# Two transformer blocks on one core: the end of the squared-relu MLP with joined norm weights, an unscaled VectorE sum, and the residual scaled a stage later

## Chip, cores and metric

One core of one Trainium2 chip. The metric is the device time of one execution in microseconds, the median of several runs; lower is better. The kernel before takes 2157.38 us (three runs, 2157.03 to 2157.44). A profile of one execution of it stands beside that.

## The reference, cut to what matters

Two blocks follow each other on 512 tokens of width 1024. The change lies where the first ends and the second begins. The first block's MLP squares a relu, its result goes through a final norm, and the second block norms that again ahead of its short convolution:

```python
    h = rmsnorm(x, norm_ffn[l])
    x = x + jnp.square(jax.nn.relu(h @ w_ff1[l])) @ w_ff2[l]
    return rmsnorm(x, final_norm)
...
            xn = rmsnorm_2(x, attn_norm[l])
            x = x + short_conv_mixer(xn, a_w_in[l], a_conv[l], a_w_out[l])
```

With s the MLP's sum per token, r1 its inverse root mean square, and fin and attn the two weight vectors (one number for each of the 1024 features), the residual that goes on is s * fin * r1, and the second norm is s * fin * attn * r1 * r2, with r2 from the mean square of s * fin * r1. So two sums of squares are wanted: that of s, and that of s * fin.

## The kernel before

Activations lie with features on partitions: x is eight tiles of 128 features by 512 tokens, f32. All products are f32 by splitting: each operand is cut into a high part (xh, wh) and the rest (xl, wl), and each chunk of 128 features takes three matmuls (lines 202 to 204). mm_T makes one product, 128 outputs by 512 tokens, in eight chunks, so 24 matmuls. Weights come as 1 MB chunks through SP's queue into four raw buffers, each chunk holding two units; prep cuts a unit into wh (ScalarE) and wl (VectorE) two units ahead of its use, into room for three units. A load goes out when a raw buffer is free, that is after the wl that read it last. PSUM has eight banks, one a product.

The framework plans the order of each engine's instructions by a simulated timeline; each engine then runs its own list in order, and waits on semaphores. So the order in the code is not always the order on an engine: matmuls of two or three products may be mixed.

The MLP runs in four groups g (lines 912 to 924). Each makes eight products f1 with relu, square and split, and then eight products f2; of each of those VectorE takes t = product * rb2 (tile rs, line 918), and GpSimd adds it to x[i] (line 919). In the last group, g = 3, more follows for each i: the square of x[i] into acc1; x[i] times fin on VectorE (line 922); the square of that into acc2; and split with attn as scale (lines 475 to 483), which gives the pair xh (ScalarE, line 120) and xl (VectorE, line 110). Squares are ScalarE's (sq), their sums GpSimd's (acc, line 107). These eight pairs XN are the right operands of the conv stage.

The conv stage (lines 947 to 973) makes products ac, ah, ab for i = 0 to 7. After the second product stats_x is emitted (lines 927 to 935: ones-matmuls ss, line 439, over acc1 and acc2, then short VectorE and ScalarE operations on 128x4 for r1 and r1 * r2), after the third bcast_x (lines 937 to 943: matmuls bc, line 455, spread two such vectors over the partitions as rb and rbx, rbb is rb squared, and GpSimd multiplies each x[i] by rbx). Then got_c, got_h and got_b take the products; x itself is read again only at the stage's end, by the ao products' sums (line 880).

Of the kernel before, what the change touches and what calls it, by code (L numbers as in the profile page):

```python
# [8 lines left out]
F32 = mybir.dt.float32  # L9
# [4 lines left out]
ALU = mybir.AluOpType  # L14
# [8 lines left out]
NEG = -1e30  # L23
FF = 4096
FF2 = 2816
# buffers: raw weights, split weights, 2 KB tiles, small tiles, pairs of tiles, tiles of the attention
N_RAW = 4
N_W = 6
N_T = 54
N_S = 10  # L30
N_T2 = 6
XA = 14
# units of weights split ahead of their use
LOOK = 2
# recurrence: products of the gates beside it, levels of decays ahead, start and pace beside the
# products, levels at which the head before is normed, levels whose product is GpSimd's
N_FILL = 3
AHEAD = 4
HGSTART = 36
HGW = (130, 76)  # L40
CS = (0, 2, 6)
MUL_POOL = (1, 3)
# attention: steps from scores to the turn and on to the values, queries ahead, order of queries
# and gates, start and pace beside the products, steps of a product at which norms go on, blocks
# of queries that GpSimd divides
LAG = 4
VLAG = 3
QL = 3
# [9 lines left out]
def tile_two_blocks(ctx: ExitStack, tc: tile.TileContext, a: dict, out: bass.AP):  # L58
    nc = tc.nc
    act, dve, pool, pe = nc.scalar, nc.vector, nc.gpsimd, nc.tensor  # L60

    cp = ctx.enter_context(tc.tile_pool(name="const", bufs=1))
# [43 lines left out]
    def tt(e, o, i0, i1, op=ALU.mult):  # L106
        e.tensor_tensor(out=o, in0=i0, in1=i1, op=op)  # L107

    def stt(o, i0, s, i1, op0, op1):
        dve.scalar_tensor_tensor(out=o, in0=i0, scalar=s, in1=i1, op0=op0, op1=op1)  # L110

    def ts(e, o, i, s1, op0, s2=None, op1=None):
        if s2 is None:
            e.tensor_scalar(out=o, in0=i, scalar1=s1, scalar2=None, op0=op0)  # L114
        else:
            e.tensor_scalar(out=o, in0=i, scalar1=s1, scalar2=s2, op0=op0, op1=op1)
# [5 lines left out]
    def pieces(t, n):  # L122
        return t.rearrange("p (b i) -> p b i", i=n)

# [1 line left out]
    chunks = {}  # L126
    plan = []

# [125 lines left out]
            return e.value  # L254

    def weave(main, side, mt, st, late=False):
        """Emits two streams side by side, each at the pace of its length on the tensor engine."""
        m = s = 0.0
        end = object()
        md = sd = False  # L260
        while not (md and sd):
            c = None
            if not sd and (md or s * mt < m * st or late and not s):
                c = next(side, end)
                if c is end:
                    sd = True
                    continue
                if c is not None:
                    s += c
                    continue  # L270
                assert not md
            c = next(main, end)
            if c is end:
                md = True
            elif s or not late:
                m += c

    def stream(jobs, hooks=()):
        """Products and what follows each; the hooks run between the first products."""
        done = []  # L280
        for n, (mm, then) in enumerate(jobs):
            done.append((then, run(mm)))
            if n < len(hooks):
                hooks[n]()
            if n + 1 >= len(hooks):
                for t, p in done:
                    t(p)
                done = []

    # plan of all weights in the order of use  # L290
    w_in = a["w_in"][0]
    plan += plan_N("zv", w_in, 0, KD, 512, 1)
    plan += plan_T("zu", w_in, 0, KD, 0, 512)
# [54 lines left out]
    plan += plan_T("bo", a["b_w_out_2"][0], 0, KD, 0, D)  # L348
    plan += plan_ffn(1)

# [1 line left out]
    ident = cp.tile([128, 128], F32, name="ident")  # L352
    make_identity(nc, ident)
    ones = cp.tile([128, 128], F32, name="ones")
# [3 lines left out]
    onesr = cp.tile([128, 128], F32R, name="onesr")  # L358
    dve.tensor_copy(onesr, ones)

    # the small vectors, a chunk of 128 to a row; the first norm's come first
    vt0 = T("vt0", (8, 128))
    nc.scalar.dma_start(out=vt0, in_=a["norm_mix"].rearrange("o (r c) -> (o r) c", c=128))
    xn = []
# [53 lines left out]
    def V(key, i=0):  # L418
        r = rows[key] + i
        return vecs[:, r:r + 1]  # L420

# [1 line left out]
    def rsqrt(m, n):  # L423
        l = SM("ln")[:, :n]
        f(l, m, AF.Ln)
# [49 lines left out]
    def split(src, g=None, alloc=None):  # L475
        h, l = (alloc or R)("xh"), (alloc or R)("xl")
        if g is None:
            act.copy(h, src)
            tt(dve, l, src, h.bitcast(F32), ALU.subtract)
        else:  # L480
            f(h, src, AF.Copy, scale=g)
            stt(l, src, g, h.bitcast(F32), ALU.mult, ALU.subtract)
        return h, l
# [2 lines left out]
        pin(act.preload_act_table_set("natural_log_exp_and_others"))  # L486

    def clamp_sig(t):
        """sigmoid of an SBUF tile that is at least -80."""
        e = T("e")  # L490
        f(e, t, AF.Exp, scale=-1.0)
        f(e, e, AF.Ln, bias=1.0)
        s = T("sg")
        f(s, e, AF.Exp, scale=-1.0)
        return s

# [1 line left out]
    x = [T("x") for _ in range(KD)]  # L498
    table()
    X = []  # L500
# [19 lines left out]
    rcol = cp.tile([128, NT], F32, name="rcol")  # L520
    nrm = {}

    # masks of the decay levels
    LV = [1, 2, 4, 8, 16]
    masks = cp.tile([128, len(LV), 64], U8, name="masks")

# [9 lines left out]
                               pattern=[[2 * h, nb], [0, h]], channel_multiplier=-1)  # L536
            pool.tensor_copy(masks[:, n, :], m)

# [1 line left out]
    gbc, bbc, sbc, wsn = T("lng"), T("lnb"), T("bs"), T("wsn")  # L540
    nc.sync.dma_start(out=gbc, in_=a["gmlp_ln_g"].to_broadcast([128, 512]))
    nc.sync.dma_start(out=bbc, in_=a["gmlp_ln_b"].to_broadcast([128, 512]))
# [56 lines left out]
            tt(pool, t, t, U[g])  # L599
            YF.append(t)  # L600

# [1 line left out]
    reset = T("reset")  # L603
    pool.memset(reset, 1.0)
    pool.memset(pieces(reset, 64)[:, :, 0:1], 0.0)
# [50 lines left out]
        heads[h] = (kq, sc, gate)  # L656

    class Core:
        """One head of the recurrence: the decays of the halving levels, scores, values."""

        def __init__(self, h):
            self.h = h
# [165 lines left out]
        yield 1000  # L828
        cores[7].done()

# [1 line left out]
    def gated(pg, py, o):  # L832
        t = T("gz")
        tt(dve, t, pg, rb)
# [56 lines left out]
    X = [residual("wo", MX, i, V("ffn", i), acc) for i in range(8)]  # L891
    close_x()

# [1 line left out]
    def stats_f():  # L895
        rf = rsqrt(mean_eps(ssq(acc.t), 1.0 / D), NT)
        nrm["rf2"] = SM("rf2")[:, :NT]
# [2 lines left out]
    def bcast_f():  # L900
        nrm["rb2"] = bcast(nrm["rf2"])

    acc1, acc2 = Acc(), Acc()
    XN = []

    def relu2(p):
        t = T("rl")
# [4 lines left out]
    for g in range(4):  # L912
        Fq = []
        stream([(mm_T("f1", X), relu2) for i in range(8)], [stats_f, bcast_f] if g == 0 else ())
        for i in range(8):
            p = run(mm_T("f2", Fq))
            t = T("rs")
            tt(dve, t, p, nrm["rb2"])
            tt(pool, x[i], x[i], t, ALU.add)
            if g == 3:  # L920
                acc1.add(x[i])
                ts(dve, x[i], x[i], V("fin", i), ALU.mult)
                acc2.add(x[i])
                XN.append(split(x[i], V("attn", i)))
    X = XN

    def stats_x():
# [9 lines left out]
    def bcast_x():  # L937
        nrm["rb"] = bcast(nrm["r12"])
        nrm["rbb"] = T("rbb")
        tt(pool, nrm["rbb"], nrm["rb"], nrm["rb"])  # L940
        nrm["rbx"] = bcast(nrm["r1"])
        for i in range(8):
            tt(pool, x[i], x[i], nrm["rbx"])


# [1 line left out]
    def conv(u, q, w):  # L947
        f(u, q, AF.Copy, scale=w(2))
        stt(u[:, 1:S], q[:, 0:S - 1], w(1), u[:, 1:S], ALU.mult, ALU.add)
# [85 lines left out]

    X, acc = conv_ffn(0, X, False)

# [1 line left out]
    open_x(XA)  # L1039
    XQ = []  # L1040

# [6 lines left out]

    bft = cp.tile([16, 1], F32, name="bft")
    nc.sync.dma_start(out=bft, in_=a["b_f_2"].rearrange("(h o) -> h o", o=1))  # L1050
    # block-diagonal ones, causal mask, selector of a head's row
    bo = T("bo", (128, 128))
    pool.memset(bo, 0.0)
    pool.memset(bo[0:64, 0:64], 1.0)
# [9 lines left out]
    id16 = cp.tile([128, 128], BF16, name="id16")  # L1064
    pool.tensor_copy(id16, ident)

    # f: log of the forget gates, summed over the tokens
    cr = xp[-1].tile([48, 512], F32R, tag="x", name="cr")
    pool.memset(cr.bitcast(F32), 0.0)
    sel = T("sel", (48, 16))  # L1070
# [24 lines left out]
    ts(dve, kqs[:, 1:2], V("qn"), -0.0625, ALU.mult)  # L1095

    class HeadNorm:
        """RMS norm over each head's 64 rows, in steps that lie apart."""

        def __init__(self, p, gk, by):  # L1100
            self.gk, self.by = gk, by
# [62 lines left out]
    gates = {}  # L1164

    def paced(mm):
        """A product; between its steps the norms of the queries before it go on."""
        n = 0
        while True:
            try:  # L1170
                c = next(mm)
            except StopIteration as e:
                return e.value
            n += 1
            if n == FIN:
                finish_norms()
            if n == START:
                start_norms()
            yield c
# [26 lines left out]
    stacks, parts = {}, []  # L1206

    def stack(h):
        """The parts of a head's queries and keys, one under the other, in steps that lie apart."""
        i, hA = divmod(h, 2)  # L1210
        qn, kn = pairs[i], KN[i]
        if hA:
            pairs.pop(i)
        u = slice(64 * hA, 64 * hA + 64)
        w = slice(64 - 64 * hA, 128 - 64 * hA)
        qa, ka, qb = (xp[-1].tile([128, 512], F32R, tag="x", name=nm(s)) for s in ("qa", "ka", "qb"))
        kb = kbs[h % len(kbs)]
        stacks[h] = (qa, ka, qb, kb)

        def high():  # L1220
            act.copy(ka[u, :], kn[u, :])
            act.copy(qa[u, :], qn[u, :])

        def low_k():
            tt(dve, kb[0:64, :], kn[u, :], ka[u, :].bitcast(F32), ALU.subtract)
            pool.tensor_copy(qb[64:112, :], selr[:, h:h + 1].bitcast(F32).to_broadcast([48, 512]))

        def low_q():
            tt(dve, qa[w, :], qn[u, :], qa[u, :].bitcast(F32), ALU.subtract)

        def twice():
            dve.tensor_copy(ka[w, :], ka[u, :].bitcast(F32))
            dve.tensor_copy(qb[0:64, :], qa[u, :].bitcast(F32))

        return [high, low_k, low_q, twice]
# [135 lines left out]
```

## Time and profile before

| | |
|---|---|
| median of three runs | 2157.38 us (2157.03 to 2157.44) |
| span of the profiled execution | 2155.2 us |
| mean granted clock of TensorE | 0.993 of full |
| TensorE matmuls busy | 2119.9 us, 98% |
| VectorE busy | 1243.4 us, 58% |
| ScalarE busy | 879.5 us, 41% |
| GpSimd busy | 522.9 us, 24% |

The profile is of one execution; its span runs from the first to the last instruction, and the measured time holds some 2 us beyond that. PE is TensorE's matmuls, PEld its weight loads, DVE is VectorE, ACT ScalarE, POOL GpSimd. Every row names line, engine, operation and the tiles written and read. Most elementwise operations go through helpers, so that one line (107 is tensor_tensor, 110 scalar_tensor_tensor, 120 activation) stands for many places, and the tile's name tells which. Times are microseconds from the span's start unless marked ns. Matmuls are pipelined: one of 0.39 us follows the last after 0.23. A small part of the matmul records is missing.

### The profile page before, as it was taken

What the parts mean: (1) busy time and instruction counts of PE and PEld (TensorE: products, weight loads), DVE (VectorE), ACT (ScalarE), POOL (GpSimd) and SP (SyncE); (2) the same over time, 40 slices, a digit from 0 to 9 for tenths busy, and PEclk for the clock granted to TensorE, in tenths of its full rate; (3) what the DMA queues carried; (4) which work ended last, traced back from release to release, by engine and by line L of the source; (5) the groups of instructions that cost most, each with busy time, mean ns of one, the idle gap of its engine ahead of it and who ended that gap; (6) DMA issues with size and microseconds to landing.
All of it is one profiled execution on the core that took longest, in us unless ns stands there. A gap on an engine that the chain in (4) does not pass through costs nothing.

```text
span 2155.2 us, 24922 instructions
## 1 busy us (share of the span) xinstructions
PE 2119.9 (98%) x9984; PEld 1739.5 (81%) x9984; DVE 1243.4 (58%) x1605; ACT 879.5 (41%) x1349; POOL 522.9 (24%) x446
## 2 busy tenths in 40 slices
PE   9999999999999999899999999999999999999999
PEld 7888777888888888688888888878877778888887
DVE  5588896555344443654555454568587755545453
ACT  6455555544323323332333232345466653323232
POOL 2537664012222222530111010020024411101000
PEclk9999999999999999999999999999999999999999
DMA  6311111232233332132322232232211112323321
GB/s 217 98 62 57 40 59 59 98 108 89 97 98 98 98 98 85 52 118 78 118 79 98 98 101 95 83 114 79 95 43 40 59 59 79 98 98 98 98 88 49
DMA packets 179180, 187.38 MB, mean 87 GB/s; under 512 B 4379, under 2 KB 169976, under 8 KB 179064
## 3 DMA queue, kind: packets, MB, share of 16 engines
q1 hardware_dynamic: 179048, 185.79, 26.6%
q8 instruction: 78, 1.28, 0.2%
q14 instruction: 38, 0.31, 0.0%
q10 hardware_dynamic: 16, 0.00, 0.0%
HBM read 183.68 MB, written 2.10 MB: 86 GB/s over the span
## 4 chain that ended last, share of the span: by engine, by line
PE 85%; DVE 7%; POOL 3%; ACT 3%; issue 2%; DMA 0%; SPq 0%; DVEq 0%; POOLq 0%; ACTq 0%
PE mm L202 25%; PE mm L203 25%; PE mm L204 25%; PE ao L1282 2%; POOL dec L107 2%; PE mn L244 1%; PE mn L243 1%; PE mn L242 1%; DVE wl L182 1%; ACT e L120 1%; DVE dec L107 1%; DVE sc L107 1%; PE pt L1270 1%; DVE e L110 1%; PE sc L1244 1%
## 5 line engine op out<-in xcount | busy, mean ns | idle before, releaser
L202 PE MATMUL mm<-xh,wh 128*128 128x512 f32 x2552 | 1006.6, 395 | 5.9 <-ACT xh L120 5.2
L203 PE MATMUL mm<-xl,wh 128*128 128x512 f32 x2552 | 999.2, 392 | 0.7 <-DVE xl L110 0.6
L204 PE MATMUL mm<-xh,wl 128*128 128x512 f32 x2552 | 998.5, 392 | 0.5 <-DVE wl L182 0.5
L181 ACT CAST wh<-raw 128x1024 fp32r<-128x1024 f32 (+2 forms) x355 | 363.5, 1025 | 783.5 <-PE mm L203 688.4
L182 DVE TENSOR_TENSOR wl<-raw,wh 128x1024 fp32r<-128x1024 f32 (+2 forms) x355 | 466.3, 1315 | 179.1 <-ACT wh L181 175.2
L202 PEld LDWEIGHTS mm<-xh,wh 128*128 128x128 f32 x2552 | 481.2, 189 | 106.9 <-ACT xh L120 6.1
L204 PEld LDWEIGHTS mm<-xh,wl 128*128 128x128 f32 x2552 | 480.6, 188 | 102.6 <-DVE wl L182 1.0
L203 PEld LDWEIGHTS mm<-xl,wh 128*128 128x128 f32 x2552 | 480.9, 188 | 100.5 <-DVE xl L110 2.0
L107 POOL TENSOR_TENSOR ua<-ua,rb 128x512 f32<-128x512 f32 x44 | 57.3, 1302 | 592.6 <-ACT ua L120 592.6
L107 DVE TENSOR_TENSOR x<-mm,x 128x512 f32<-128x512 f32 x64 | 44.1, 690 | 153.3 <-PE mm L204 153.3
L107 POOL TENSOR_TENSOR dec<-sc 128x256 f32<-128x256 f32 x96 | 89.5, 958 | 41.5 <-ACT kq L120 20.9
L107 DVE TENSOR_TENSOR a<-mm,rb 128x512 f32<-128x512 f32 x44 | 30.4, 691 | 103.5 <-PE mm L204 103.5
L107 POOL TENSOR_TENSOR acc<-acc,sq 128x512 f32<-128x512 f32 x42 | 62.8, 1495 | 103.9 <-ACT sq L120 82.0
L107 POOL TENSOR_TENSOR rl<-rl 128x512 f32<-128x512 f32 x32 | 49.0, 1532 | 129.3 <-ACT rl L120 129.3
L107 DVE TENSOR_TENSOR sg<-mm,ua 128x512 f32<-128x512 f32 x44 | 30.4, 690 | 84.3 <-POOL ua L107 81.8
L114 POOL TENSOR_SCALAR pe<-pe,rs 128x128 f32<-128x128 f32 (+1 forms) x32 | 31.1, 971 | 188.9 <-DVE rs L1262 184.1
L107 POOL TENSOR_TENSOR x<-x,rs 128x512 f32<-128x512 f32 x32 | 48.6, 1518 | 113.8 <-DVE rs L107 113.8
L110 DVE SCALAR_TENSOR_TENSOR xl<-x,vecs,xh 128x512 fp32r<-128x512 f32 x48 | 63.5, 1327 | 15.3 <-ACT xh L120 15.2
L110 DVE SCALAR_TENSOR_TENSOR ua<-a,convs,ua 128x511 f32<-128x511 f32 x88 | 65.8, 747 | 4.8 <-ACT ua L120 3.3
L242 PE MATMUL mn<-wh,xh 128*128 128x512 f32 x160 | 63.5, 404 | 0.0
L120 ACT ACTIVATE ua<-ua 128x512 f32<-128x512 f32 x44 | 27.8, 632 | 86.5 <-DVE ua L110 86.4
L243 PE MATMUL mn<-wl,xh 128*128 128x512 f32 x160 | 62.5, 391 | 0.0
(249 smaller groups left out, 2070.6 us busy)
## 6 DMA issues: line engine op xcount, KB each, us to landing
raw<-in_ffn_w_up_dram SPq DMA_DIRECT2D x44, 1024.0 KB
raw<-in_w_ff_dram SPq DMA_DIRECT2D x32, 1024.0 KB
raw<-in_w_in_dram SPq DMA_DIRECT2D x26, 1024.0 KB
raw<-in_ffn_w_down_dram SPq DMA_DIRECT2D x18, 1024.0 KB
raw<-in_a_w_in_dram SPq DMA_DIRECT2D x12, 1024.0 KB
raw<-in_w_kvf_dram SPq DMA_DIRECT2D x8, 1024.0 KB
raw<-in_b_w_qg_dram SPq DMA_DIRECT2D x8, 1024.0 KB
raw<-in_w_up_b_dram SPq DMA_DIRECT2D x4, 1024.0 KB
```

Source lines behind the costliest of these rows:

```text
L107: e.tensor_tensor(out=o, in0=i0, in1=i1, op=op)
L110: dve.scalar_tensor_tensor(out=o, in0=i0, scalar=s, in1=i1, op0=op0, op1=op1)
L114: e.tensor_scalar(out=o, in0=i, scalar1=s1, scalar2=None, op0=op0)
L120: act.activation(out=o, in_=i, func=func, scale=scale, bias=bias, **kw)
L181: act.copy(hi, src)
L182: ins = dve.tensor_tensor(out=lo, in0=src, in1=hi.bitcast(F32), op=ALU.subtract)
L202: pe.matmul(ps, lhsT=lh, rhs=rh, start=start, stop=False)
L203: pe.matmul(ps, lhsT=lh, rhs=rl, start=False, stop=False)
L204: pe.matmul(ps, lhsT=ll, rhs=rh, start=False, stop=stop_)
L242: pe.matmul(pss[j], lhsT=xh[:, t0], rhs=wh[:, kk, :], start=(k + kk == 0), stop=False)
L243: pe.matmul(pss[j], lhsT=xh[:, t0], rhs=wl[:, kk, :], start=False, stop=False)
L1282: pe.matmul(o[64 * hA:64 * hA + 64, tb * 128:(tb + 1) * 128], lhsT=v[j][h // 8][:, (h % 8) * 64:(h % 8) * 64 + 64], rhs=et[:, j * 128:(j + ...
```

## The change

The weights fin and attn are multiplied once into a 128x8 tile, fa. In the last group the sum x[i] + t goes to VectorE; the pair for the conv stage is split from that unscaled sum with fa as scale, ahead of the squares; acc2 takes its square with fin as ScalarE's scale, and x[i] itself stays unscaled. In bcast_x one scalar_tensor_tensor on VectorE multiplies x[i] by fin and by rbx, in place of GpSimd's multiplication by rbx alone. The rest of the diff removes comments and docstrings.

```diff
     acc1, acc2 = Acc(), Acc()
     XN = []
+    fa = cp.tile([128, 8], F32, name="fa")
+    tt(dve, fa, vecs[:, rows["fin"]:rows["fin"] + 8], vecs[:, rows["attn"]:rows["attn"] + 8])
...
             tt(dve, t, p, nrm["rb2"])
-            tt(pool, x[i], x[i], t, ALU.add)
+            tt(dve if g == 3 else pool, x[i], x[i], t, ALU.add)
             if g == 3:
+                XN.append(split(x[i], fa[:, i:i + 1]))
                 acc1.add(x[i])
-                ts(dve, x[i], x[i], V("fin", i), ALU.mult)
-                acc2.add(x[i])
-                XN.append(split(x[i], V("attn", i)))
+                acc2.add(x[i], V("fin", i))
...
         for i in range(8):
-            tt(pool, x[i], x[i], nrm["rbx"])
+            stt(x[i], x[i], V("fin", i), nrm["rbx"], ALU.mult, ALU.mult)
```

## Rows read from the trace of the kernel before

**Rows 1.** The page's first part: busy us (share of span) xinstructions, by engine

```profile
PE 2119.9 (98%) x9984; PEld 1739.5 (81%) x9984; DVE 1243.4 (58%) x1605; ACT 879.5 (41%) x1349; POOL 522.9 (24%) x446
```

**Rows 2.** TensorE's waits, whole span: us in total, times, longest us

```profile
PE mm L202 <- ACT xh L120: 5.2, 2, 3.7
...
PE ss L439 <- POOL acc L107: 2.7, 1, 2.7
```

**Rows 3.** Stretches: us, busy PE PEld DVE ACT POOL, PEclk, DMA share, GB/s

```profile
893.00:928.00 35.00, 25.82 (x95) 19.55 (x93) 19.11 (x32) 11.35 (x19) 13.49 (x10) 0.76 0.04 11
928.00:1000.00 72.00, 72.00 (x320) 59.67 (x320) 38.98 (x45) 20.38 (x24) 20.75 (x14) 1.00 0.39 126
...
915.00:920.00 5.00, 5.00 (x18) 4.29 (x18) 3.35 (x15) 0.82 (x4) 0.64 (x1) 0.50 0.01 2
```

**Rows 4.** Timeline of VectorE, rs of group 2 and first of group 3

```profile
769.32 0.69 DVE L107 TENSOR_TENSOR rs<-mm,rb 128x512 f32<-128x512 f32 x1 [4.70 <-PE mm L204]
...
798.33 0.69 DVE L107 TENSOR_TENSOR rs<-mm,rb 128x512 f32<-128x512 f32 x1 [2.24 <-PE mm L204]
803.77 0.69 DVE L107 TENSOR_TENSOR rs<-mm,rb 128x512 f32<-128x512 f32 x1 [2.24 <-PE mm L204]
...
856.36 0.69 DVE L107 TENSOR_TENSOR rs<-mm,rb 128x512 f32<-128x512 f32 x1 [4.70 <-PE mm L204]
```

**Rows 5.** Timeline of TensorE: conv stage's start, first broadcast, ss a stage later

```profile
890.61 0.39 PE L202 MATMUL mm<-xh,wh 128*128 128x512 f32 x1
...
926.37 0.22 PE L455 MATMUL bc<-identr,rh 128*128 128x128 f32 x1
...
1090.91 0.95 PE L439 MATMUL ss<-ones,acc 128*128 128x1 f32 x8
```

**Rows 6.** Chain that ended last, one product of group 3: start, us, what

```profile
893.70 0.69 DVE rs L107
894.45 2.20 POOL x L107
896.68 0.64 ACT sq L120
897.34 1.60 DVE x L114
...
899.50 0.71 ACT xh L120
...
901.48 0.69 DVE rs L107
```

**Rows 7.** Groups by tile, whole span: ns min/median/max, first and last start

```profile
L181 ACT CAST wh<-raw x355: 299/1053/1058, 3.7 to 2135.1; 128x1024 fp32r<-128x1024 f32 x169, 128x512 fp32r<-128x512 f32 x4, 128x768 fp32r<-128x768 f32 x4, 128x128 fp32r<-128x128 f32 x1
L182 DVE TENSOR_TENSOR wl<-raw,wh x355: 283/1225/2367, 7.7 to 2136.6; 128x1024 fp32r<-128x1024 f32 x169, 128x512 fp32r<-128x512 f32 x4, 128x768 fp32r<-128x768 f32 x4, 128x128 fp32r<-128x128 f32 x1
...
L110 DVE SCALAR_TENSOR_TENSOR xl<-x,vecs,xh x48: 736/1339/1784, 507.0 to 1789.3; 128x512 fp32r<-128x512 f32 x48
L107 DVE TENSOR_TENSOR xl<-rl,xh x32: 683/693/693, 558.1 to 851.0; 128x512 fp32r<-128x512 f32 x32
...
L110 DVE SCALAR_TENSOR_TENSOR u<-ch,vecs,u x16: 743/749/1653, 931.8 to 1040.0; 128x511 f32<-128x511 f32 x8, 128x510 f32<-128x510 f32 x8
```

**Rows 8.** Timeline of VectorE, then GpSimd: one product at the conv stage's end

```profile
1058.93 0.69 DVE L107 TENSOR_TENSOR x<-mm,x 128x512 f32<-128x512 f32 x1 [1.61 <-PE mm L204]
...
1060.98 1.78 DVE L110 SCALAR_TENSOR_TENSOR xl<-x,vecs,xh 128x512 fp32r<-128x512 f32 x1
1064.37 0.69 DVE L107 TENSOR_TENSOR x<-mm,x 128x512 f32<-128x512 f32 x1 [1.60 <-PE mm L204]
...
1060.48 1.73 POOL L107 TENSOR_TENSOR acc<-acc,sq 128x512 f32<-128x512 f32 x1 [3.71 <-ACT sq L120]
```

**Rows 9.** Timeline of GpSimd, then VectorE: last acc, end of the statistics

```profile
914.38 1.27 POOL L107 TENSOR_TENSOR acc<-acc,sq 128x512 f32<-128x512 f32 x1 [1.08 <-issue]
...
920.36 0.16 DVE L107 TENSOR_TENSOR rl<-r,rh 128x4 fp32r<-128x4 f32 x1
```

## Prediction, made before the change was run

> **What bounds the kernel now.** I read the page's first part, then the waits of TensorE, then busy time by stretch, and only there the single instructions. TensorE is busy 98% of the span [rows 1], so an edit on another engine is worth only what TensorE idles or loses in clock because of it. Two waits of the whole list sit at the changed place: matmuls wait 5.2 us for xh, and the sums (ss) 2.7 us for GpSimd's acc [rows 2]. By stretch, 893 to 928 us is the one hole here: TensorE busy 25.82 of 35 us at a mean granted clock of 0.76, against 72.00 of 72 us at 1.00 in the next stretch; from 915 to 920 the grant is 0.50, the 1.2 GHz level, just after an engine that had stood and waited [rows 3]. So the hole costs idle time and half speed behind it.
>
> **Size of the hole.** Where does the last product of the MLP really end? In the group before (g = 2) the rs of the first product starts at 769.32 and that of the eighth at 803.77, 34.45 us later, with 5.44 us between the last two, each paced by TensorE [rows 4]. In g = 3 the first rs starts at 856.36, so the eighth product is ready by about 890.8; the trace has a matmul that opens a group at 890.61 [rows 5], which I take as the start of the conv stage. From there to the first broadcast matmul at 926.37 [rows 5] TensorE does three products (ac, ah, ab of i = 0: 3 x 8 chunks x 3 = 72 matmuls) and two sets of ss. At full clock a product is 5.44 us [rows 4], and one set of ss takes 0.95 us in the same place a stage later [rows 5]. Needed: 3 x 5.44 + 2 x 0.95 = 18.2 us. Taken: 35.8 us. The hole is 17.5 us.
>
> **Why it is there.** The chain of waits shows one product: rs on VectorE 0.69, x add on GpSimd 2.20, square on ScalarE 0.64, x times fin on VectorE 1.60, xh 0.71, then xl; the next rs starts 7.78 us after the one before, because VectorE is in order and its next rs stands behind this xl [rows 6]. The step is 7.78 us where a product needs 5.44. Seven steps put the last XN some 7 x 2.34 = 16 us behind TensorE.
>
> **The change, part by part.**
> *The x add moves from GpSimd to VectorE (8 times).* Removed: 2.20 us and one hand-over per step [rows 6]. Added: a tensor_tensor with two SBUF inputs of the same shape, 0.69 us (the row of xl<-rl,xh) [rows 7].
> *fin is no longer multiplied into x, and xh comes straight from the sum.* Removed from the chain: a square 0.64 and the multiplication 1.60 [rows 6]. Both squares remain but lie behind xh; ScalarE has the room (per product wh 1.05, xh 0.71 and two squares of 0.64, 3.0 us of 5.44) [rows 6, 7].
> *The new step.* rs 0.69 + add 0.69 + xh 0.71 + xl 0.74 to 1.78 [rows 6, 7] + three hand-overs of about 0.07 = 3.0 to 4.1 us serial. With the split of the weights (wl 1.23 median) in the gaps, VectorE's own sum is 0.69 + 0.69 + 1.23 + 1.78 = 4.4 us at most by these, under 5.44. The conv stage's own end does nearly this already: add, xl of 1.78 beside a GpSimd sum, and the next add after 5.44 us with VectorE idle 1.60 us waiting for TensorE [rows 8]. One rs of 0.69 more fits into that idle time. So the last XN is there at 890.8 + 4.1 = 894.9.
> *Does TensorE notice?* At 894.9 it has had 7 of 8 chunks of three products ready, 63 of 72 matmuls or 14.3 us of work from 890.6, so it need not stop for the last chunk.
> *The sums.* sq, sq after xh by 894.4, then two GpSimd adds of 1.27 [rows 9] to 1.73 [rows 8]: done by 897.3. From the end of the last acc to the end of rl the chain now takes 920.52 - 915.65 = 4.87 us [rows 9]: rl at 902.2, before the three products end at 906.9. Covered, if ss stands no earlier in TensorE's order than about 897.
> *x gets fin and rbx on VectorE in the next stage (8 scalar_tensor_tensor in place of 8 GpSimd multiplications).* Not in the trace on x; bounds are the stt on u, 0.749 median to 1.653 [rows 7], so 6.0 to 13.2 us of VectorE, and I take 6.0, since GpSimd loses 8 multiplications there and is mostly idle. They wait for rbx; behind them in the queue may stand got_c, got_h and wl. VectorE is busy 38.98 of 72 us in that stretch [rows 3], so there is room for 6 to 13. c and ch only free PSUM (8 banks, three in use by products), x is read again a stage later, and a unit of weights is split two units ahead, 10.9 us before its use, of which wh and wl take under 2.5: a delay of some 8 us is hidden. So it costs nothing; nor can it gain, because TensorE is full in that stretch already [rows 3]. If that cover is gone, up to 5 us beyond it plus half clock.
> *fa, one 128x8 product,* lies 300 us ahead beside full TensorE: under 0.2 us, hidden. SP's queue gets no load more; a load is issued when wl frees its buffer, and none of these is later than now. GpSimd's queue only gets shorter, so the u multiplications start earlier.
>
> **A rule against the change.** In the trace GpSimd's acc runs 1060.48 to 1062.21, and an xl that starts at 1060.98 ends at 1062.76, 0.55 us after it, taking 1.78 where its shortest is 0.736 [rows 7, 8]. The Trainium skill, "SBUF — State Buffer", section "Who interferes with whom", says that a VectorE instruction with two SBUF inputs and a GpSimd instruction that reads SBUF exclude each other, the later one waiting out the whole of the first. By this rule the moved add and the eight new multiplications are of the kind that can be locked out; the trace agrees for xl, and the next section prices it as a rival.
>
> **Sum.** The profiled span is 2155.2 us; the median of the three runs is 2157.38, so 2.2 us lie outside the span, and the change doesn't touch them. 2157.4 - 17.5 = 2139.9 us (span about 2137.7).
>
> **Rivals.**
> *A new wait on TensorE (2147.2).* All engines are in order and the planner writes TensorE's order: ss or the broadcast may stand where acc or rl is not yet there. Priced by what one such wait does now: 2.7 us [rows 2], and half clock until about 922.5, where some 14 matmuls at twice 0.227 and the ss at half speed cost 4.6: 7.3 us of the 17.5. For it: two sums are added per product, not one. Against: the ends of the other stages have no such wait [rows 2].
> *Lock-out of VectorE (2146.9).* If add, wl and xl meet both GpSimd sums in full, the step is 0.69 + 0.69 + 1.23 + 0.74 + 2 x 1.73 = 6.8 us. The last XN then comes at 856.4 + 7 x 6.8 + 4.1 = 908.1; TensorE is through the other 63 matmuls at 905, idles 3 and is at half speed for the rest, about 7 in all. For it: xl above. Against: the sums run after xh, when add is over.
> *The multiplications of x delay the weights (2146).* 8 x 1.653 ahead of wl, some 5 us over the cover and a little clock.
> *No difference (2157).* The chain keeps a step of 7.2 to 8.4 us for a reason that I don't see; each 0.1 us of step is 0.7 us of time.
> *Slower (2166).* VectorE itself becomes the bound: with the add locked out by one whole GpSimd sum and every other operation at its longest, rs 0.69 + add 0.69 + 1.73 + an unfilled wait for wh and xh 1.05 + 0.71 + xl 1.78 + wl 2.37 = 9.0 us [rows 6 to 8]. From a step of 7.78 it loses, and from 8.4 measurably; at 9.0 it is 7 x 1.2 = 8.5 us. For it: wl does reach 2.37 [rows 7]. Against: the conv stage's end, where the same operations leave VectorE idle 1.60 a product [rows 8].
>
> **How the numbers follow.** Forecast 0.65, with a range of its own of 2137 to 2143 (the planner orders all later work anew; hand-overs). New wait 0.16, lock-out 0.08, delayed weights 0.03, no difference 0.04, slower 0.04. A measurement of this kernel tells about 0.2% (4.3 us) from no change. So faster 0.92, same 0.04, slower 0.04. To leave out no more than 2 in 10 the range takes in the rivals near 2147: 2137 to 2148.
>
> **What would show it.** Right: in the eight products of g = 3 the rs steps 5.44 us and waits for TensorE, xl ends within about 4 us of each rs; TensorE has no wait for xh and a clock of 1.00 from 893 on; the first broadcast matmul stands near 909 in place of 926.4; everything behind it is as before, some 18 us earlier. Wrong: a step above 5.44, a wait of ss for acc or of bc for rl with half clock behind it, or a wait for wl between 910 and 930. The prediction falls if TensorE's wait has moved rather than gone.

## Result: 2139.5 us, and the profile after

The changed kernel takes 2139.53 us (median of four runs, 2138.79 to 2142.39) against 2157.20 us of the kernel before (four runs, 2156.31 to 2157.44). The ratio is 0.9922, 95% interval 0.9908 to 0.9936: faster by 17.7 us, where 17.5 had been forecast (2139.9).

The page's first part of the changed kernel answers to [rows 1]:

```profile
PE 2111.0 (99%) x9984; PEld 1734.8 (81%) x9984; DVE 1240.9 (58%) x1614; ACT 879.4 (41%) x1349; POOL 500.4 (23%) x430
```

TensorE runs the same 9984 matmuls and is busy 8.9 us less. VectorE is busy 2.5 us less although it has nine instructions more, and GpSimd has 16 fewer. TensorE's waits over the whole span (columns as in [rows 2]):

```profile
PE lv L733 <- DVE dec L107: 8.3, 4, 2.4
...
PE mm L202 <- ACT xh L478: 0.7, 1, 0.7
```

Both entries of [rows 2] are gone, that for xh of line 120 (5.2 us) and that of ss for acc (2.7 us), and none has come in their place. What is left stands in other stages. The same stretches as in [rows 3]:

```profile
893.00:928.00 35.00, 35.00 (x172) 29.50 (x172) 23.00 (x42) 11.25 (x17) 7.08 (x5) 1.00 0.28 91
915.00:920.00 5.00, 5.00 (x24) 4.14 (x23) 5.00 (x8) 1.48 (x2) 0.00 (x0) 1.00 0.14 44
```

The hole is closed: 35.00 of 35 us busy at a clock of 1.00, where 25.82 at 0.76 stood before; from 915 to 920 the grant is 1.00 and no longer 0.50. In that same piece VectorE is busy 5.00 of 5 us, most of it with the eight late multiplications, and TensorE runs on.

Now the last two products of the last group on VectorE, with the wl before them (start, us, engine, line, operation, tiles, idle time before and its releaser):

```profile
886.55 1.55 DVE L182 TENSOR_TENSOR wl<-raw,wh 128x1024 fp32r<-128x1024 f32 x1 [0.70 <-ACT wh L181]
888.03 0.68 DVE L107 TENSOR_TENSOR rs<-mm,rb 128x512 f32<-128x512 f32 x1
888.74 1.07 DVE L107 TENSOR_TENSOR x<-x,rs 128x512 f32<-128x512 f32 x1
890.66 0.75 DVE L110 SCALAR_TENSOR_TENSOR xl<-x,fa,xh 128x512 fp32r<-128x512 f32 x1 [0.85 <-ACT xh L120]
892.13 1.55 DVE L182 TENSOR_TENSOR wl<-raw,wh 128x1024 fp32r<-128x1024 f32 x1 [0.71 <-ACT wh L181]
893.60 0.68 DVE L107 TENSOR_TENSOR rs<-mm,rb 128x512 f32<-128x512 f32 x1
894.31 1.07 DVE L107 TENSOR_TENSOR x<-x,rs 128x512 f32<-128x512 f32 x1
896.24 0.75 DVE L110 SCALAR_TENSOR_TENSOR xl<-x,fa,xh 128x512 fp32r<-128x512 f32 x1 [0.85 <-ACT xh L120]
```

and GpSimd beside it:

```profile
885.73 1.30 POOL L107 TENSOR_TENSOR acc<-acc,sq 128x512 f32<-128x512 f32 x1 [2.03 <-ACT sq L120]
887.29 1.97 POOL L107 TENSOR_TENSOR acc<-acc,sq 128x512 f32<-128x512 f32 x1 [0.27 <-ACT sq L120]
...
896.86 2.54 POOL L107 TENSOR_TENSOR acc<-acc,sq 128x512 f32<-128x512 f32 x2 [2.02 <-ACT sq L120]
```

The step is 5.57 us (888.03 to 893.60), not 7.78 [rows 6]. It does not wait for TensorE: its two idle pieces, 0.85 and 0.71, wait for ScalarE's xh and wh. From the last rs to the end of the last xl it is 3.39 us (893.60 to 896.99).

The first matmul of the conv stage, what follows on TensorE, and then on VectorE:

```profile
890.77 0.39 PE L202 MATMUL mm<-xh,wh 128*128 128x512 f32 x1
...
901.65 1.84 PE L439 MATMUL ss<-ones,acc 128*128 128x1 f32 x16
908.94 0.22 PE L455 MATMUL bc<-identr,rh 128*128 128x128 f32 x1
```

```profile
907.78 0.16 DVE L107 TENSOR_TENSOR rl<-r,rh 128x4 fp32r<-128x4 f32 x1
...
913.55 5.39 DVE L110 SCALAR_TENSOR_TENSOR x<-x,vecs,rb 128x512 f32<-128x512 f32 x8 [0.70 <-ACT rb L458]
```

The first broadcast matmul starts at 908.94, where 926.37 stood [rows 5]. From the stage's first matmul to the broadcast it is 908.94 - 890.77 = 18.17 us. The sums ss stand behind two products of the conv stage, not three (901.65 - 890.77 = 10.88 us, two products of 5.44): the third lies between ss and the broadcast.

**A cleaner measure of the place.** The first rs of the last group starts at 856.36 before [rows 4] and at 856.52 after. Planner and recurrence move that point by some 3 us from kernel to kernel (below), so I count from it. Up to the first broadcast it is 926.37 - 856.36 = 70.01 us before and 908.94 - 856.52 = 52.42 after: 17.59 us gained at the place, practically the whole of the difference in time. TensorE in these two stretches, before and then after (us, busy PE, PEclk, DMA share, GB/s):

```profile
856.36:926.37 70.01, 60.83 (x241) 0.88 0.14 46
856.52:908.94 52.42, 52.42 (x241) 1.00 0.28 87
```

With the same 241 matmuls on record, 9.18 us of the 17.59 were idle time, and 8.41 were matmuls that ran slower under the lower clock. The spans of the two profiled executions differ by 16.8 us only, for the changed kernel reaches the place 0.16 us later and takes 0.63 us more behind it.

In the same way the last xl ends 59.83 us after that point before, at 916.19 by this row of the kernel before,

```profile
914.89 1.30 DVE L110 SCALAR_TENSOR_TENSOR xl<-x,vecs,xh 128x512 fp32r<-128x512 f32 x1 [1.31 <-ACT xh L120]
```

and 896.99 - 856.52 = 40.47 us after. All kernels by this measure, the last two columns in us from the first rs of the last group; each ratio is to runs of the kernel before that were taken with it (medians 2157.19 to 2158.34):

| kernel | median us | ratio to before (95%) | last xl ends | first broadcast |
|---|---|---|---|---|
| before | 2157.2 | 1 | 59.83 | 70.01 |
| after | 2139.53 | 0.9922 (0.9908 to 0.9936) | 40.47 | 52.42 |
| e1_add_only | 2151.38 | 0.9973 (0.9963 to 0.9983) | 51.68 | 62.95 |
| e2_split_only | 2141.33 | 0.9923 (0.9907 to 0.9940) | 42.38 | 52.42 |
| e6_split_alone | 2139.87 | 0.9916 (0.9900 to 0.9933) | 42.38 | 52.42 |
| e5_scale_after_rbx | 2140.20 | 0.9919 (0.9905 to 0.9934) | 40.46 | 52.42 |
| e3_old_scaling | 2146.05 | 0.9946 (0.9932 to 0.9961) | 45.64 | 56.37 |
| e4_late_split | 2142.22 | 0.9929 (0.9912 to 0.9945) | 44.81 | 53.02 |
| d1_more_per_step | 2140.52 | 0.9922 (0.9907 to 0.9937) | 42.26 | 52.42 |
| d2_more_per_step | 2147.67 | 0.9954 (0.9939 to 0.9969) | 50.10 | 59.41 |
| d4_more_per_step | 2163.02 | 1.0023 (1.0014 to 1.0033) | 62.90 | 72.19 |
| b3_more_stt | 2140.28 | 0.9920 (0.9906 to 0.9935) | 40.44 | 52.42 |

Six kernels reach 52.42 to the hundredth: that is TensorE without a gap. A last xl up to 42.4 us costs nothing. At 44.8 it costs 0.6, and the kernels beyond that lose what their last xl is past some 43 us, within 2 us (more where ss waits as well).

### The profile page after: what moved, and what is told of

It reads as the page before. It is cut to its first block, busy times and chain, and to the rows that moved or that the text cites. A ratio compares the mean times of both kernels' runs of the same rounds, so it can differ in the third digit from the quotient of the medians.

```text
span 2138.4 us, 24917 instructions
## 1 busy us (share of the span) xinstructions
PE 2111.0 (99%) x9984; PEld 1734.8 (81%) x9984; DVE 1240.9 (58%) x1614; ACT 879.4 (41%) x1349; POOL 500.4 (23%) x430
## 4 chain that ended last, share of the span: by engine, by line
PE 86%; DVE 6%; ACT 2%; POOL 2%; issue 2%; DMA 0%; SPq 0%; DVEq 0%; POOLq 0%; ACTq 0%
PE mm L202 25%; PE mm L203 25%; PE mm L204 25%; PE ao L1284 2%; POOL dec L107 2%; PE mn L243 1%; PE mn L244 1%; PE mn L242 1%; ACT e L120 1%; DVE wl L182 1%; DVE dec L107 1%; PE pt L1272 1%; DVE sc L107 1%; DVE e L110 1%; PE sc L1246 1%
## 5 line engine op out<-in xcount | busy, mean ns | idle before, releaser
L244 PE MATMUL mn<-wh,xl 128*128 128x512 f32 x160 | 60.9, 392 | 0.0
L107 DVE TENSOR_TENSOR dec<-dec,kq 128x512 f32<-128x512 f32 x56 | 53.1, 955 | 9.3 <-ACT dec L120 9.3
```

The costliest lines, as they stand in the source:

```text
L244: pe.matmul(pss[j], lhsT=xl[:, t0], rhs=wh[:, kk, :], start=False, stop=(k + kk == nk - 1))
```

## The experiments

The theory: one chain in a step of 7.8 us is the hole, and the change shortens that chain. Open were which of the three edits does it, how much room the new step has, and whether the rivals (a wait that moves on, lock-out, late multiplications, VectorE as the bound) are real prices.

**The sum alone on VectorE** (the kernel before with one line):

```diff
-            tt(pool, x[i], x[i], t, ALU.add)
+            tt(dve if g == 3 else pool, x[i], x[i], t, ALU.add)
```

> The kernel before with one edit: in the last group the sum x + t is VectorE's; fin is still multiplied into x ahead of the split. Theory A (what counts is the step of the serial chain rs, sum, square, times fin, xh, xl, and TensorE loses what the last XN comes later than about 900 us, where the first two products of the conv stage are used up): the step falls from 7.78 by 2.20 - 0.72 to about 6.3 us, the last xl is ready near 906.5 and not 916.2, and TensorE loses 6.5 to 9 us in place of 17.5: 2146 to 2149 us. Theory B (GpSimd's slow sum is what costs): nearly all of the gain, 2140 to 2142. Theory C (the sum doesn't matter, only the unscaled split): 2155 to 2157.

Measured 2151.38: a third of the gain in time, and 7.06 of the 17.59 us at the place (its first rs is at 858.14, 1.6 us later than in the changed kernel). That lies between the ranges of theories A and C and in none; A had the step at 6.3 us and the last xl near 906.5, and they are about 6.6 and 909.82. One product on VectorE, with the last multiplication by fin:

```profile
898.41 0.69 DVE L107 TENSOR_TENSOR x<-x,rs 128x512 f32<-128x512 f32 x1
900.16 1.51 DVE L114 TENSOR_SCALAR x<-x,vecs 128x512 f32<-128x512 f32 x1
903.09 1.26 DVE L110 SCALAR_TENSOR_TENSOR xl<-x,vecs,xh 128x512 fp32r<-128x512 f32 x1 [1.43 <-ACT xh L120]
904.27 0.68 DVE L107 TENSOR_TENSOR rs<-mm,rb 128x512 f32<-128x512 f32 x1
...
906.43 0.49 DVE L114 TENSOR_SCALAR x<-x,vecs 128x512 f32<-128x512 f32 x1 [0.76 <-ACT sq L120]
```

TensorE, the waits at the end of the stage:

```profile
903.06 0.73 PE L202 MATMUL mm<-xh,wh 128*128 128x512 f32 x2 [0.85 <-ACT xh L120]
...
908.10 1.87 PE L439 MATMUL ss<-ones,acc 128*128 128x1 f32 x8 [2.50 <-POOL acc L107]
```

The sum takes 0.69 in place of 2.20 [rows 6] and the step falls to about 6.6 us (897.70 to 904.27), but x times fin, xh and xl still follow one another, and the wait of ss for acc stays, at 2.5 us. Half the clock comes with it: 0.50 from 910 to 915.

**The split alone, sum on GpSimd** (the changed kernel with the sum moved back):

```diff
-            tt(dve if g == 3 else pool, x[i], x[i], t, ALU.add)
+            tt(pool, x[i], x[i], t, ALU.add)
```

> The changed kernel with one part undone: the sum x + t of the last group stays on GpSimd; the split is from the unscaled sum, with fin scaled in later. Theory A (step of the serial chain): GpSimd now has the sum and two acc per product with a wait for xh and the square between them, 2.2 + 1.35 + 1.3 + 1.3 = about 6.15 us a step; the last xl near 904; TensorE loses 4 to 5.5 us: 2144 to 2145 us (2140 if GpSimd isn't held up and the step stays at 5.5). Theory B (GpSimd's sum is what costs): little gained, 2150 or more. Theory C (only the split counts): 2139.5.

Measured 2141.33, and 52.42 at the place: the whole gain without the sum's move. The expectation of a loss of some 5 us fell; it had GpSimd's sum locked out as before. The trace shows it at 1.29 us in each product, not 2.20, and a step of 5.44:

```profile
889.80 0.68 DVE L107 TENSOR_TENSOR rs<-mm,rb 128x512 f32<-128x512 f32 x1
...
894.58 0.74 DVE L110 SCALAR_TENSOR_TENSOR xl<-x,fa,xh 128x512 fp32r<-128x512 f32 x1
895.24 0.68 DVE L107 TENSOR_TENSOR rs<-mm,rb 128x512 f32<-128x512 f32 x1
...
899.75 0.75 DVE L110 SCALAR_TENSOR_TENSOR xl<-x,fa,xh 128x512 fp32r<-128x512 f32 x1 [3.83 <-ACT xh L120]
```

```profile
892.24 1.29 POOL L107 TENSOR_TENSOR x<-x,rs 128x512 f32<-128x512 f32 x1
```

The wl of this step starts at 893.43, when the sum is nearly over. The chain of one product, from rs to the end of xl, just fills a step (889.80 to 895.32): xl stands behind wl and right ahead of the rs of the next product, and starts without a wait, since the sum and xh are ready by then; the two squares' sums fall into the next step. The broadcast itself stands at 910.54, 1.6 us later than in the changed kernel, but so does the first rs (858.12 for 856.52): in the recurrence, at 367 us, a matmul waits 2.89 us for osh, a tile of that stage, where the changed kernel's waits 1.34. The planner ordered that stage otherwise; the place is the same.

**The split alone, and the residual scaled by two operations:**

```diff
-            tt(dve if g == 3 else pool, x[i], x[i], t, ALU.add)
+            tt(pool, x[i], x[i], t, ALU.add)
...
-            stt(x[i], x[i], V("fin", i), nrm["rbx"], ALU.mult, ALU.mult)
+            tt(pool, x[i], x[i], nrm["rbx"])
+            ts(dve, x[i], x[i], V("fin", i), ALU.mult)
```

> Of the changed kernel only the split from the unscaled sum with fin*attn, and fin as ScalarE's scale for the second sum of squares: the sum stays on GpSimd, and x[i] gets rbx on GpSimd and then fin on VectorE, both after the broadcast. Theory: this part alone carries the gain, 2139.5 to 2142, step of VectorE 5.44, last xl near 900.5. Rival: the parts help each other, and with both others undone GpSimd carries eight sums, sixteen square sums and eight multiplications at the place and becomes late: 2144 or more, with TensorE waiting for acc or for u.

Measured 2139.87 and 52.42. With both other edits undone the time is the same, so the split from the unscaled sum, with fin as the scale of the second square, carries the gain by itself.

**The sum on VectorE, the residual scaled by two operations** (only the second part of the diff above):

> The changed kernel, but the joint multiplication is taken apart behind the broadcast: GpSimd multiplies x[i] by rbx as in the kernel before, and VectorE then by fin (16 operations in place of 8, both tied to rbx so that none can be moved into the MLP). Theory: the place is hidden, so whether it is one operation or two costs nothing; the last xl ends at 897 to 900.5, the first broadcast is near 909 to 911, the time 2139.5 to 2141.5. Rival: GpSimd's eight multiplications, which cannot read while VectorE works with two operands, run late and hold up the multiplications by u behind them, and TensorE waits at the ab or ao products: 2143 or more with a new wait of TensorE after 930.

Measured 2140.20 and 52.42; no wait of TensorE behind 930. The last multiplication by fin ends at 930.25, 11.3 us later than the joint form's last, and nobody notices. One operation or two, on VectorE or on GpSimd: all hidden.

**The same two operations in the other order:**

```diff
-            stt(x[i], x[i], V("fin", i), nrm["rbx"], ALU.mult, ALU.mult)
+            ts(dve, x[i], x[i], V("fin", i), ALU.mult)
+            tt(pool, x[i], x[i], nrm["rbx"])
```

> The changed kernel with its last part undone: in the conv stage x is multiplied by fin on VectorE (tensor_scalar) and by rbx on GpSimd, 8 each, in place of the eight scalar_tensor_tensor. If the late scaling is hidden wherever it is done: 2139.5 us within 0.2%. If GpSimd's eight multiplications, which hold up its product of u in the kernel before, cost something behind the end of the MLP: 2 to 5 us more.

Measured 2146.05, above both ranges expected: 6.5 us of the gain are lost, and not for the reason tested. The multiplication by fin now depends on nothing of the conv stage, and the planner puts it back into the MLP's step:

```profile
900.41 1.52 DVE L114 TENSOR_SCALAR x<-x,vecs 128x512 f32<-128x512 f32 x1
901.85 0.68 DVE L107 TENSOR_TENSOR rs<-mm,rb 128x512 f32<-128x512 f32 x1
902.56 1.07 DVE L107 TENSOR_TENSOR x<-x,rs 128x512 f32<-128x512 f32 x1
904.48 0.75 DVE L110 SCALAR_TENSOR_TENSOR xl<-x,fa,xh 128x512 fp32r<-128x512 f32 x1 [0.85 <-ACT xh L120]
```

At the place that costs 56.37 - 52.42 = 3.95 us: 0.66 us of waiting for xh, 0.36 for acc, and a granted clock of 0.69 from 908 to 913. Another 3.07 us lie ahead of the first rs (859.59), again in the recurrence, with a wait for osh of 2.91 as in e2_split_only and a clock from 300 to 400 us of 0.95, where e2_split_only has 0.98. I put that part down to the planner's order there, which the edit does not touch by itself. What the joint form does here is to tie the multiplication to rbx; e5, which ties it without joining, does as well.

**The split emitted behind the squares:**

```diff
-                XN.append(split(x[i], fa[:, i:i + 1]))
                 acc1.add(x[i])
                 acc2.add(x[i], V("fin", i))
+                XN.append(split(x[i], fa[:, i:i + 1]))
```

> The changed kernel with the split emitted behind the two squares, as it stands in the kernel before; the sum and its scale stay as changed. Theory A (TensorE loses what the last xl ends later than about 899.6 us): ScalarE now has square, wh and square ahead of xh, about 1.9 us more in the serial chain, but the step stays near that of the products, 5.4 to 5.8 us, and the last xl ends at 898 to 901: 2139.5 to 2141.5 us. If the place of the split is a part of the gain by itself: 2143 or more.

Measured 2142.22, between the two ranges expected; at the place 0.60 us more. The middle steps are 6.2 to 6.3 us and not 5.4 to 5.8, with xl beside a GpSimd sum:

```profile
892.61 1.79 DVE L110 SCALAR_TENSOR_TENSOR xl<-x,fa,xh 128x512 fp32r<-128x512 f32 x1
894.32 0.68 DVE L107 TENSOR_TENSOR rs<-mm,rb 128x512 f32<-128x512 f32 x1
```

The last product catches up (4.16 us), so only 0.6 us is left of it, 0.35 of that a wait of ss for acc. The order of split and squares is worth little here; this kernel is the nearest of all to the edge of the room.

**VectorE loaded further in each step.** One, two or four more operations on x in each product of the last group, which leave x as it is:

```diff
+                for _ in range(2):
+                    stt(x[i], x[i], 1.0, x[i], ALU.mult, ALU.max)
```

> The changed kernel with one more scalar_tensor_tensor on VectorE in each step of the last group, between the sum and the split. By the run with two (step 5.93 us, last xl ending at 907.5, 8.1 us lost) one fits nearly whole into the waits of VectorE's step: step 5.6 to 5.8, last xl at 898.5 to 901, 2139.5 to 2141.5 us. If loss goes with the number of added operations: 4 us, 2143.5.

> The changed kernel with two more scalar_tensor_tensor on VectorE in each step of the last group, between the sum and the split (x = max(1.0 x, x), which leaves x as it is). Theory A: the step of 5.57 us grows by 2 x 0.7 to about 7.0 us, the last xl from 897.0 to about 908, TensorE loses 8 to 10 us: 2147 to 2150 us. If the cover were the 14.3 us of three products that the prediction counted, so that lateness only counts from 905, the loss is 3 to 5 us: 2143 to 2145. Rival (VectorE's queue has slack and the operations fill its waits): 2139.5.

> The changed kernel with four more scalar_tensor_tensor on VectorE in each step of the last group. VectorE has no wait left with two (5.93 us a step); two more of 0.65 to 1.1 us make 7.2 to 8.1 us a step, the last xl ends at 918 to 923, TensorE loses 18 to 23 us: 2158 to 2163 us, which is the kernel before or slower. This is the rival on the slower side of the prediction (VectorE as the bound, losing from a step of 7.78), made on purpose. If the loss saturates because other work of TensorE moves forward: 2150 to 2154.

One more (0.7 us in the first two products, 1.66 in the others) costs nothing: 2140.52 and 52.42. Two fill VectorE: from the fourth step to the sixth it has no idle time, and a step is 5.93 us. (The second step, 8.38, holds waits of 0.80 for xh and 1.82 for wh.) The kernel takes 2147.67 us and loses 6.99 at the place. TensorE in it:

```profile
901.10 0.73 PE L202 MATMUL mm<-xh,wh 128*128 128x512 f32 x2 [1.14 <-ACT xh L120]
...
906.75 1.22 PE L202 MATMUL mm<-xh,wh 128*128 128x512 f32 x2 [3.67 <-ACT xh L120]
```

Four make the step 7.15 us at the end, 7.96 on the mean (856.45 to 912.17 in seven steps; before it is 7.56, 856.36 to 909.27), and the kernel slower than before: 2163.02, ratio 1.0023 (1.0014 to 1.0033). TensorE waits for xh four times, 14.5 us in all:

```profile
904.42 1.22 PE L202 MATMUL mm<-xh,wh 128*128 128x512 f32 x2 [5.17 <-ACT xh L120]
911.53 1.22 PE L202 MATMUL mm<-xh,wh 128*128 128x512 f32 x2 [4.18 <-ACT xh L120]
```

At the place this profile loses 2.2 us against the kernel before (72.19 to 70.01), and its execution took 2159.86; the median of its ten runs lies 3 us above that, which no trace here explains. So the forecast's slower rival exists, but it takes some 3.8 us of VectorE more per product to make it.

**Twenty-four more operations behind the eight late multiplications:**

```diff
             stt(x[i], x[i], V("fin", i), nrm["rbx"], ALU.mult, ALU.mult)
+            for _ in range(3):
+                stt(x[i], x[i], 1.0, x[i], ALU.mult, ALU.max)
```

> The changed kernel with 24 more scalar_tensor_tensor on x (x = max(1.0 x, x), which leaves x as it is) behind the eight that scale it, 18 us more of VectorE in the conv stage's first 30 us. If a delay of some 8 us of the weights' split is all that is hidden, as the prediction says, and the operations stand ahead of wl in the queue: a stall of about 10 us and half clock behind it, 2150 or more. If the planner lets each wl through between them in time: no loss, 2139.5, and then the eight operations of the change cost nothing with much room to spare.

Measured 2140.28 and 52.42. TensorE, VectorE and the clock in two stretches (columns as in [rows 3]):

```profile
915.00:930.00 15.00, 15.00 (x68) 12.43 (x67) 15.00 (x24) 3.90 (x4) 0.00 (x0) 1.00 0.07 23
930.00:942.00 12.00, 12.00 (x55) 9.94 (x54) 10.82 (x17) 2.12 (x2) 7.46 (x1) 1.00 0.04 9
```

VectorE is busy for 15 us without a gap, and TensorE is full at a clock of 1.00. The 24 operations take 14.9 us. The planner lets each wl slip in between them, at 922.83, 928.84, 934.25 and 939.00. The first two of these come 3.0 and 5.8 us later than in the changed kernel (919.46 and 922.71 there, with a first rs 0.36 us earlier), and the weights are still in time. A longer delay of wl was not made.

## Why the prediction was right, and where its steps were not

The sum held because its largest term, the hole, was read off TensorE alone: 17.5 us to gain. Measured are 17.59 at the place and 17.67 in the time. The 18.2 us that the stretch needs are confirmed: it takes 18.17 in the changed kernel, and six kernels without a gap at the place have the same distance to the hundredth. That the whole hole closes hung on every later step staying under its cover. They did, but several with other sizes than argued, and two of these errors, the new step and the cover, go against the forecast. That what was left sufficed was in part luck.

- *The new step.* The serial chain from rs to the end of xl, 3.0 to 4.1 us, measures 3.39. VectorE's own sum, 4.4 us at most, is 0.68 + 1.07 + 0.75 + 1.55 = 4.05. Wrong is "steps 5.44 us and waits for TensorE": the step is 5.57, by the prediction's own list a sign of being wrong, because VectorE in order waits twice for ScalarE (0.85 and 0.71) and so does not use its room. From the first product of a group to the eighth TensorE takes 34.45 us [rows 4], so the eighth was there at 890.97 and its rs came 2.6 us later. The last XN was therefore at 896.99, not 894.9.
- *The cover.* The prediction had TensorE through 63 matmuls of three products before it needs the last chunk, to 905. In the trace two products stand ahead of ss, so it is 42 matmuls, 9.5 us, to about 900. d2 shows it: its last xl, 50.10 us from the first rs, is 1.5 us past a cover to 905 (48.6 us). But TensorE stands already from 903.08 on, 45.7 us from the first rs, though it had waited 1.14 us before that, and 7 us are lost. The forecast stood with 2 to 3 us to spare, where it believed in 10.
- *The sums.* Forecast done at 897.3, measured 899.40; ss starts at 901.65, so 2.2 us are left. From the end of the last acc to the end of rl it is 8.5 us and not 4.87, for ss waits its turn behind two products, and VectorE takes two wl in between. rl ends at 907.94 and the broadcast starts at 908.94: 1.0 us of room. Of the steps priced here this is the tightest in the new kernel, and the likeliest place for the forecast's rival of a new wait on TensorE; here it did not come.
- *Lock-out of VectorE.* It is there, in other places than priced. xl runs free in seven of eight products (0.75), but the add takes 1.07 for 0.69, wl 1.55 for 1.23 and acc 1.97 for 1.29. The rival added both GpSimd sums in full to the step (6.8 us); in the trace acc, wl, acc and add stand in a row from 885.73 to 889.81, and the waiting falls partly on GpSimd, which has the time.
- *The late multiplications.* Eight in 5.39 us, forecast 6.0; hidden, as said. In b3 14.9 us more of such work cost nothing. That a delay of the weights of some 8 us is hidden stays untested: b3 delays a wl by 5.8.
- *fa.* One product of 1.19 us at 61.1 us in the first stage, not 300 us ahead and not under 0.2; hidden all the same.
- *The part that matters.* The prediction let the sum's move and the split share the gain. The move alone gives 7.06 us of 17.59 (e1), the split alone everything (e2, e6), and on top of the split the move gives no time, only room: the last xl ends 1.9 us sooner (40.47 for 42.38). The 2.20 us of GpSimd's sum was itself a result of the old order, where wl ran beside it; with the split moved up it takes 1.29, and the chain it stands in fits the step. So the 2.20 us per step that the prediction counts as removed were not needed. What within the split is worth how much no run separates. It is not the multiplication alone: d1 puts an operation as long (1.66 us) back between sum and split and loses nothing.

## What to carry to other kernels

Size a gain from the bounding engine alone (what it took from one fixed point to another, less what its work needs), and use the chains of the other engines only to ask whether they stay under the cover; here their sizes were off by 2 to 5 us and the gain by 0.1. Look for the cover in the bounding engine's actual order of instructions, since a planner may put the next consumer a whole product earlier than the code suggests. An operation that is to leave a tight stage must be tied to something of the later stage, or the planner may put it back, as in e3.

## What the hardware showed that was not expected

**Of two elementwise operations on VectorE and GpSimd, one can wait out the other.** The multiplication by fin takes 0.49 us in e1 when it starts with GpSimd idle, and 1.51 (900.16) when it starts 0.19 us after a GpSimd sum; in the kernel before it takes 1.60 [rows 6]. GpSimd beside these two, in e1 and in the kernel before:

```profile
899.97 1.41 POOL L107 TENSOR_TENSOR acc<-acc,sq 128x512 f32<-128x512 f32 x1 [2.75 <-ACT sq L120]
```

```profile
897.38 1.26 POOL L107 TENSOR_TENSOR acc<-acc,sq 128x512 f32<-128x512 f32 x1 [0.74 <-ACT sq L120]
```

GpSimd's sum of x takes 2.20 in the kernel before, starting at 894.45 [rows 6], 0.15 us after a wl, and 1.29 in e2. In the changed kernel acc starts at 887.29 inside a wl that ends at 888.10, and runs to 889.26; the add starts at 888.74 and ends at 889.81, 0.55 us after it. So the operation of such a pair that waits is finished about its own free duration, less 0.13 to 0.2 us, after the other ends, and either engine can be the one that waits. The Trainium skill, "SBUF — State Buffer", section "Who interferes with whom", states this exclusion for VectorE operations with two SBUF inputs, and for tensor_scalar in a mode with two ports. The rows of add, wl and xl agree with the first (1.07, 1.55 and in e4 1.79 us), and the multiplication by fin behaves as the second. That the later of the two waits, as the prediction took it from there, holds by the starts in these profiles for the pairs above that start 0.15 us and more apart. It does not for the multiplication by fin in the kernel before: it starts at 897.34, 0.04 us ahead of acc (897.38), and yet acc takes its free 1.26 us and the multiplication waits. What the prediction missed is its consequence: moving one operation moves the price to another, here in part to GpSimd's acc, which has the time.

**A short wait can be dearer than it looks.** In e1 waits of 0.85 and 0.61 us and then of 2.50 for acc are followed by a granted clock of 0.50, the 1.2 GHz level, from 910 to 915; in e3 0.66 and 0.36 us of waiting and 0.69 from 908 to 913. Of the 3.95 us that e3 loses at the place, 1.02 is the waiting that the list names. Not every wait is so dear: e4's 0.35 us for acc leaves the clock at 1.00 from 900 to 913, and e4 loses 0.60 us.
